# Eight chunk products of a pair of heads, issued head by head or with the two heads alternating

## The chip, the cores and the metric

The kernel runs on one core of a Trainium2 chip, in one launch. The metric is the device time of an execution in microseconds (us); a kernel's time is the median of its runs. The engines are TensorE (PE for its matmuls, PEld for its weight loads), VectorE (DVE), ScalarE (ACT), GpSimd (POOL) and SyncE (SP), which issues most DMAs. All arithmetic is in f32; the large products split their operands into two parts and issue three matmuls for one.

## What is computed

A network of two kinds of blocks over one sequence of 512 tokens with 1024 features: two blocks with a feed-forward part, a mixer of window attention and a convolution, another feed-forward part and a gate; then two blocks whose mixer has three branches side by side: a gated delta rule (6 heads), a sparse attention (6 heads) and a stick-breaking attention (4 heads). The change touches the gated delta rule alone. Its reference, cut to what matters (H = 6 heads, D = 64 features, chunks of C = 64 tokens, so n = 8 chunks):

```python
def gated_deltanet(q, k, v, z, a, b_logit, conv_w, a_log, dt_bias, norm_w):
    ...
    lower = jnp.where(strict, jnp.einsum('bhncd,bhnsd->bhncs', k_beta, k) * decay, 0.0)
    rhs = jnp.concatenate([v * beta[..., None], k_beta * jnp.exp(g)[..., None]], axis=-1)
    sol = lax.linalg.triangular_solve(lower, rhs, left_side=True, lower=True, unit_diagonal=True)
    u, w = jnp.split(sol, 2, axis=-1)
    attn = jnp.einsum('bhncd,bhnsd->bhncs', q, k) * decay

    def step(state, xs):
        q_i, k_i, u_i, w_i, g_i, a_i = xs
        v_new = u_i - jnp.einsum('bhcd,bhde->bhce', w_i, state)
        o_i = (jnp.einsum('bhcd,bhde->bhce', q_i * jnp.exp(g_i)[..., None], state)
               + jnp.einsum('bhcs,bhse->bhce', a_i, v_new))
        ...
    _, o = lax.scan(step, jnp.zeros((bsz, H, D, D), f32), xs)
```

Everything before the scan is independent for each chunk and each head.

## The kernel before

Features lie on partitions and tokens on columns, so a tile is [128, 512]. The class `Gdn` works on pairs of heads, j = 0, 1, 2: the first head of a pair on partitions 0 to 63, the second on 64 to 127, and the eight chunks side by side in 64 columns each. A product of one chunk of one head is therefore 64x64 times 64x64: it uses the upper or the lower half of TensorE's rows, and writes the same half of the partitions of one PSUM tile. `chunks8` (line 1368) issues such a product for every chunk of both heads, 16 in all; this text calls the 16 products a block. It is called from five places:

- `swap` (line 1460) transposes each head's chunks by a product with the identity. `cols` calls it for v, `pre` for k, and `gdn_mix` for the output of the scan.
- `pre` (line 1544) makes two blocks: U, the products of the chunk's keys with each other, and AT, those of queries and keys. VectorE multiplies both by the decay (line 1546).
- `mms` (line 1551) is called three times by `inverse`, for one level of the doubling of a triangular inverse: px, py and pyt. VectorE takes each result up (lines 1596, 1599, 1602).
- The end of `inverse` (line 1629) multiplies the inverse TT with the right-hand sides, which ScalarE copies out of PSUM (line 1630).

For a pair of heads that is 10 blocks, for the three pairs 30, and for the two calls of the mixer 60 blocks or 960 products. The last level of the inverse (`quarters`, line 1611) and the scan (lines 1643 to 1653) don't use `chunks8`; both issue the two heads in turn. In the scan each step has two such products for the state and two for the output.

The work beside this is large products of 128x128 by 128x512 (lines 259 to 261, `mm3`), for the next columns of the input projection, and the chain of the stick-breaking attention (lines 1169 to 1184). The program writes them as generators and takes steps from them between the small products (`pace`, `sparse`, `fill`, lines 737 to 782), so many for each block. A scheduler then sets the final order on each engine by when it estimates operands to be ready. `mms` hands the last of its 16 products to `pace`; this is the second head's last chunk in either order. Each weight tile of the large products comes by DMA on SyncE's queue and is split by ScalarE (line 232, wH) and VectorE (line 233, wL).

Of the kernel before, what the change touches and what calls it, by code (L numbers as in the profile page):

```python
# [16 lines left out]
PSUM = bass.MemoryType.PSUM  # L17
# [32 lines left out]
BLK = 16  # L50
# [15 lines left out]
class Vecs:  # L66
    """Column directory of the per-partition vectors."""
# [49 lines left out]
class Net:  # L117
# [15 lines left out]
    @contextmanager  # L133
    def phase(self, **tags):
        """Scratch: rotating [128, 512] tiles, so many of each tag. Phases nest."""
        old = self.tags, getattr(self, "tp", None)
        with self.tc.tile_pool(name="ph", bufs=1) as pool:
            self.tp = pool
            self.tags = {**old[0], **{k: v if isinstance(v, str) else (pool, v) for k, v in tags.items()}}
            yield  # L140
        self.tags, self.tp = old

    @contextmanager
    def psum(self, **tags):
        """PSUM banks, so many of each tag; or the tags that one goes round."""
# [60 lines left out]
    def weights(self, sources):  # L206
        """The [128, 1024] chunks of all weights, in the order of use."""
# [29 lines left out]
    def w(self):  # L237
        """The next 128-column tile of the weights."""
# [7 lines left out]
    def wraw(self, n):  # L246
        """The next n chunks of the weights as they are."""
# [15 lines left out]
    def mm2(self, out, l, r, **flags):  # L263
        """A narrow product in two halves of its rows, side by side in the array."""
# [9 lines left out]
    def lin(self, name, xs, tag="lin"):  # L274
        """The next product."""
# [6 lines left out]
    def lead(self, name, n, tag="lin", gain=None, norm=None, at=8, between=None):  # L282
        """The input of a step, its first products side by side, and the norm of the input."""
# [51 lines left out]
    def rstd(self, tiles, n, scale=1.0, adds=SQ_DVE):  # L335
        """1/sqrt(mean(x^2)+eps) over the features of x = scale * tiles: a row on every partition."""
# [17 lines left out]
    def rn(self, acc, n, scale=1.0):  # L354
        """By token, 1/sqrt of the mean over the partitions."""
# [8 lines left out]
    def rows(self, rn):  # L364
        """[128, 4] by token as a row on every partition."""
        return self.rows_end(*self.rows_in(rn))
# [48 lines left out]
    def rope_tables(self, pos, inv, sgn):  # L415
        """cos and signed sin of pos * inv, features on partitions."""
# [24 lines left out]
    def rope(self, ps, cos, sin, half, tag="q", tmp="t"):  # L441
        """ps * cos + swap(ps) * sin, the swap within each 32 partitions."""
# [9 lines left out]
    def mixer1(self, i):  # L452
# [7 lines left out]
        # taps by fours: their weights on the diagonals of [4 x 32, 32], a group of 32 features after the other  # L460
# [8 lines left out]
        for j in range(4):  # L469
# [6 lines left out]
            # the tile's groups of 32 features, 0 to 3 tokens late  # L476
# [19 lines left out]
        # in parts, stacked: [high, low] of a head against [high, high] of its keys  # L496
# [16 lines left out]
        def conv(j):  # L513
            """The convolution of tile j on the tensor engine, four taps at a time."""
# [134 lines left out]
    def ple(self, pT, gain, norm, last=False):  # L649
        """The gate's product, and beside it the tokens' rms-normalised projection with its gain."""  # L650
# [46 lines left out]
    def final_out(self, gain, out):  # L697
        """The last norm, by token."""
# [38 lines left out]
    def pace(self, inst, **rates):  # L737
        """Steps of the work that runs beside the current one, so many of each kind, but not ahead of
        the instruction of LAG calls before."""
# [11 lines left out]
    def sparse(self, cost):  # L751
        """Small products of a cost were issued: as many large ones belong beside them."""
# [7 lines left out]
    def fill(self, kind, n=1):  # L760
        """n steps of a kind, or all that are left."""
# [11 lines left out]
    def need(self, done, kind):  # L773
        """Steps of a kind until done."""
# [9 lines left out]
    def by_token(self, y):  # L784
        """PSUM: the tokens of y on partitions, [token, (block, feature)]."""
# [119 lines left out]
    def norm2_in(self, i, fin):  # L905
        """The input of the second block's mixer; after the first block, its last norm too."""
# [4 lines left out]
        def gates(gain):  # L911
            """Their few columns in four groups, each a fourth of the features."""
# [13 lines left out]
        def norm():  # L926
# [13 lines left out]
            # of the two norms together: (mean of the second's square + eps) / first's^2  # L940
# [9 lines left out]
    def rsqrt_ln(self, x, n, scale):  # L950
        """1/sqrt(scale * x + eps): exp of the logarithm, and one Newton step."""
# [10 lines left out]
    def head_norm(self, *args):  # L962
        """out = src / rms(src) over each 64 columns."""
# [16 lines left out]
    def to_mix(self, o, nt):  # L980
        """A token block, transposed."""
# [12 lines left out]
    def values(self, name, xs, rs):  # L994
        """The next columns, by token."""
# [58 lines left out]
    def nsa_split(self, d):  # L1054
        """Queries and keys in parts, stacked: [high, low] of a head against [high, high] of its keys."""
# [29 lines left out]
    def compress(self, i, d):  # L1085
        """The hidden units of the compressed keys and values."""
        nc = self.nc
        hids = []
        for nm in ("kc", "vc"):
            src = d[nm]  # L1090
            # pairs of tokens, with the positions' vectors in front (first half) and behind (second half)
# [34 lines left out]
    def compress2(self, d, w2):  # L1126
        """The keys and values from the hidden units."""
        nc, hids = self.nc, d["hids"]
        # each head's own part of the products, zero elsewhere: keys of two heads, values of four and of two query heads
# [17 lines left out]
    def sb(self, i, d, cr, G):  # L1147
        """Keys on partitions: log of the stick by a triangular product, then exp."""
# [48 lines left out]
    def nsa(self, i, d, G, mix, w2):  # L1197
# [44 lines left out]
        def add(n, po, f):  # L1242
            """A branch's part of the sum, and after the last one its norm."""
# [22 lines left out]
        def scores(n, br, hd):  # L1266
            """Selected (all blocks) and window (all tokens)."""
# [100 lines left out]
def chunks8(f):  # L1368
    """f of (a head's partitions, a chunk's columns), for every chunk of a pair of heads."""
    for _, s in H2:  # L1370
        for c in range(8):
# [3 lines left out]
class Gdn:  # L1375
    """Gated delta rule, in pairs of heads: on partitions a head's features or the tokens of a chunk (2 x 64)."""
# [12 lines left out]
    def gates_in(self, p):  # L1389
        """Gates, beta and the decay from a, by token."""  # L1390
# [14 lines left out]
        # softplus, cumulative over each chunk  # L1405
# [513 lines left out]
```

## Time and profile before

| | us |
|---|---|
| median of 3 runs | 3790.53 |
| lowest and highest run | 3789.84, 3797.76 |
| span of the profiled execution | 3791.1 |
| TensorE busy (matmuls) | 3723.9 |
| VectorE busy | 2311.5 |
| ScalarE busy | 1563.9 |

The profiled execution is told by its span, first instruction to last; it lies 0.6 us above the median of the runs. The first mixer of the second kind runs its gated delta rule from about 2060 to 2425 us of the span, the second from about 2940 to 3295.

How to read the rows further down: a group by line gives the line, the engine, the operation, what it writes and reads (out<-in), the shape and the number of records, then busy time, the mean length of one record in ns and the idle time ahead of it with what ended it. A timeline row gives the start in us, how long the row lasts, engine, line, operation, names, shape and the count of records in the row; a bracket tells of idle time ahead of it and who ended that. A row that holds several records lasts from the first start to the last end. One f32 matmul leaves two records, so 16 products are x32; a large product in the split type leaves one.

### The profile page before, as it was taken

Reading aid. Unit: us, or ns where it says so; the run is one execution under the profiler, and the core shown is the slowest. Engines: PE = TensorE matmul, PEld = TensorE weight load, DVE = VectorE, ACT = ScalarE, POOL = GpSimd, SP = SyncE. Lnnn points to the kernel's source line nnn. Section 1 sums busy time; section 2 is a strip of 40 time slices with the busy share of each in tenths; the row PEclk is TensorE's granted clock in tenths of the full one; section 3 lists DMA queues with packets and bytes.
Section 4 is the critical chain, followed back from the end, with each engine's and each line's share of the span. In section 5 each row is a group of like instructions: output and inputs, shape, how many; then the busy total and the mean of one; then the engine's idle time right before and its main releaser. Section 6 shows DMA issues by size and latency. Waiting matters only on the chain. (4 is left out here: it accounts for less than half of the span.)

```text
span 3791.1 us, 53948 instructions
## 1 busy us (share of the span) xinstructions
PE 3723.9 (98%) x20946; PEld 2919.5 (77%) x20946; DVE 2311.5 (61%) x4820; ACT 1563.9 (41%) x2974; POOL 147.2 (4%) x150
## 2 busy tenths in 40 slices
PE   9999999999999999999999999999999999999998
PEld 7888757888888885688887777778887777778887
DVE  5445556444743445753448876675667786676667
ACT  4233344333532334532345344553445344554345
POOL 1000000000100000100001000000001000000001
PEclk9999999999999998999999998999999999999999
DMA  3223312222322242122232111122323111122232
GB/s 132 99 95 101 106 40 89 95 100 95 100 95 100 95 127 64 52 98 100 95 100 94 68 40 68 40 100 95 100 95 134 51 40 62 46 90 100 95 100 84
DMA packets 97152, 329.85 MB, mean 87 GB/s; under 512 B 11008, under 2 KB 14976, under 8 KB 96896
## 3 DMA queue, kind: packets, MB, share of 16 engines
q1 hardware_dynamic: 90144, 311.96, 24.9%
q10 hardware_dynamic: 5472, 10.25, 0.8%
q0 software_dynamic: 1280, 4.20, 0.3%
q8 instruction: 164, 2.69, 0.3%
q14 instruction: 92, 0.75, 0.1%
HBM read 317.97 MB, written 8.39 MB: 86 GB/s over the span
## 5 line engine op out<-in xcount | busy, mean ns | idle before, releaser
L232 ACT CAST wH<-raw 128x512 fp32r<-128x512 f32 x1116 | 691.3, 620 | 1421.9 <-PE pgu L260 451.2
L233 DVE TENSOR_TENSOR wL<-raw,wH 128x512 fp32r<-128x512 f32 x1116 | 791.2, 710 | 590.4 <-ACT wH L232 558.2
L259 PE MATMUL pgu<-xH,wH 128*128 128x512 f32 x1408 | 549.5, 391 | 9.7 <-ACT wH L232 5.9
L260 PE MATMUL pgu<-xL,wH 128*128 128x512 f32 x1408 | 551.2, 391 | 6.1 <-DVE xL L313 6.1
L261 PE MATMUL pgu<-xH,wL 128*128 128x512 f32 x1408 | 550.7, 391 | 0.0
L259 PE MATMUL pd<-H,wH 128*128 128x512 f32 x1056 | 410.8, 389 | 0.0
L260 PE MATMUL pd<-L,wH 128*128 128x512 f32 x1056 | 410.8, 389 | 0.0
L261 PE MATMUL pd<-H,wL 128*128 128x512 f32 x1056 | 410.8, 389 | 0.0
L259 PEld LDWEIGHTS pgu<-xH,wH 128*128 128x128 f32 x1408 | 265.3, 188 | 65.2 <-ACT wH L232 5.9
L260 PEld LDWEIGHTS pgu<-xL,wH 128*128 128x128 f32 x1408 | 266.3, 189 | 62.2 <-DVE xL L313 6.7
L261 PEld LDWEIGHTS pgu<-xH,wL 128*128 128x128 f32 x1408 | 266.2, 189 | 55.4 <-DVE wL L233 0.2
L259 PE MATMUL pup<-xH,wH 128*128 128x512 f32 x704 | 274.8, 390 | 2.2 <-DVE h L895 1.2
L261 PE MATMUL pup<-xH,wL 128*128 128x512 f32 x704 | 274.0, 389 | 0.0
L260 PE MATMUL pup<-xL,wH 128*128 128x512 f32 x704 | 273.9, 389 | 0.0
L260 PEld LDWEIGHTS pd<-L,wH 128*128 128x128 f32 x1056 | 198.2, 188 | 41.1
L259 PEld LDWEIGHTS pd<-H,wH 128*128 128x128 f32 x1056 | 198.2, 188 | 41.1
L261 PEld LDWEIGHTS pd<-H,wL 128*128 128x128 f32 x1056 | 198.2, 188 | 41.1
L348 POOL TENSOR_TENSOR ssum<-ssum,sq 128x512 f32<-128x512 f32 x72 | 110.6, 1536 | 2674.7 <-ACT sq L347 2673.3
L259 PEld LDWEIGHTS pup<-xH,wH 128*128 128x128 f32 x704 | 132.1, 188 | 31.5 <-DVE h L895 2.0
L261 PEld LDWEIGHTS pup<-xH,wL 128*128 128x128 f32 x704 | 132.1, 188 | 27.6
L260 PEld LDWEIGHTS pup<-xL,wH 128*128 128x128 f32 x704 | 132.1, 188 | 27.1
L1344 DVE SCALAR_TENSOR_TENSOR y<-x,vecs,y 128x511 f32<-128x511 f32 (+1 forms) x176 | 131.3, 750 | 17.1 <-ACT y L1341 14.3
(568 smaller groups left out, 6108.0 us busy)
## 6 DMA issues: line engine op xcount, KB each, us to landing
raw<-ffn SPq DMA_DIRECT2D x395, 512.0 KB, 3.2
raw<-w_in SPq DMA_DIRECT2D x82, 512.0 KB, 3.2
raw<-w_out SPq DMA_DIRECT2D x40, 512.0 KB, 3.2
raw<-w_ple_gate SPq DMA_DIRECT2D x40, 512.0 KB, 3.2
away<-h ACTq DMA_DIRECT2D x16, 256.0 KB, 2.1
raw<-cmp SPq DMA_DIRECT2D x8, 512.0 KB, 3.3
h<-away POOLq DMA_DIRECT2D x16, 256.0 KB, 5.1
h<-xT SPq DMA_DIRECT2D x8, 256.0 KB, 6.5
```

What stands on the lines that cost most here:

```text
L232: nc.scalar.copy(H, r)
L233: nc.vector.tensor_tensor(L, r, H.bitcast(F32), OP.subtract)
L259: nc.tensor.matmul(ps, w[0], x[0], start=first, stop=False)
L260: nc.tensor.matmul(ps, w[0], x[1], start=False, stop=False)
L261: nc.tensor.matmul(ps, w[1], x[0], start=False, stop=last)
L348: (nc.vector if k >= adds else nc.gpsimd).tensor_tensor(acc, acc, q, OP.add)
L1344: nc.vector.scalar_tensor_tensor(y[:, s:], x[:, :T - s], w[:, f * 3 + tap:f * 3 + tap + 1], y[:, s:], OP.mult, OP.add)
```

## The change

`chunks8` swaps its two loops: the chunk becomes the outer one and the head the inner one. Each of the 960 products is still issued, with the same operands and the same output, and the first and the last product of a block are the same as before. The rest of the diff takes out comments and docstrings and moves later lines by one, so line 1551 becomes 1552 and so on.

```diff
 def chunks8(f):
-    """f of (a head's partitions, a chunk's columns), for every chunk of a pair of heads."""
-    for _, s in H2:
-        for c in range(8):
+
+
+    for c in range(8):
+        for _, s in H2:
             f(s, slice(c * 64, c * 64 + 64))
```

In the built order, the rows of a block read alike before and after, since the names and shapes of both heads' products are the same; 16 products in a row are one row. Where the scheduler sets other work between them, it shows. On TensorE, at the first pair of heads of the first mixer, at the end of `inverse` (puw are the right-hand sides times the inverse, psk and pv columns of the input projection), there stands before:

```order
L261 MATMUL psk<-xH,wL 128x512
L259 MATMUL psk<-xH,wH 128x512
L1629 MATMUL puw<-vb,TT 64x64 x16
L1629 MATMUL puw<-TT,kbg 64x64 x16
L260 MATMUL psk<-xL,wH 128x512
L261 MATMUL psk<-xH,wL 128x512
```

and now:

```order
L261 MATMUL psk<-xH,wL 128x512
L259 MATMUL psk<-xH,wH 128x512
L1630 MATMUL puw<-vb,TT 64x64
L260 MATMUL psk<-xL,wH 128x512
L1630 MATMUL puw<-vb,TT 64x64 x15
L1630 MATMUL puw<-TT,kbg 64x64 x16
L261 MATMUL psk<-xH,wL 128x512
```

One large product has moved between the first product of the block, which is the first head's, and the second, which is now the second head's. VectorE writes TT's last quarter for the first head and for the second head in two instructions (line 1625).

On TensorE, at the second pair of heads of the first mixer, the same products among the stick-breaking attention's (sbz); before:

```order
L261 MATMUL pnsa<-xH,wL 128x512
L1629 MATMUL puw<-vb,TT 64x64 x7
L1182 MATMUL sbz<-SH_17996,cr 128x384
L1629 MATMUL puw<-vb,TT 64x64 x9
L1629 MATMUL puw<-TT,kbg 64x64
L1182 MATMUL sbz<-SL_17999,cr 128x384
L1182 MATMUL sbz<-SHL_17997,cr 128x256 x2
```

and now:

```order
L261 MATMUL pnsa<-xH,wL 128x512
L1630 MATMUL puw<-vb,TT 64x64 x11
L1182 MATMUL sbz<-SH_17996,cr 128x384
L1630 MATMUL puw<-vb,TT 64x64 x5
L1630 MATMUL puw<-TT,kbg 64x64
L1182 MATMUL sbz<-SL_17999,cr 128x384
L1182 MATMUL sbz<-SHL_17997,cr 128x256 x2
```

The block is cut at the same instruction of the attention, but four products later. Cuts of this kind are in both orders at nearly the same places: 68 runs of such products before, 70 now. On TensorE, at the first block of `mms` in the first mixer, nothing but the line numbers changes; now:

```order
L259 MATMUL pqkv<-xH,wH 128x512
L1515 MATMUL row<-RS,sel 128x512 x2
L1552 MATMUL px<-T,UA 64x64 x16
L1515 MATMUL row<-RS,sel 128x512 x2
L260 MATMUL pqkv<-xL,wH 128x512
```

The orders of SyncE and GpSimd are the same as before; on VectorE and ScalarE a few instructions near such cuts change places.

## Rows read from the trace of the kernel before

**Rows 1.** Page, parts 1 and 2: busy us of each engine; TensorE's clock in tenths

```profile
PE 3723.9 (98%) x20946; PEld 2919.5 (77%) x20946; DVE 2311.5 (61%) x4820; ACT 1563.9 (41%) x2974; POOL 147.2 (4%) x150
...
PEclk9999999999999998999999998999999999999999
```

**Rows 2.** Groups by line and shape, TensorE: busy us, mean ns | idle before

```profile
L1460 PE MATMUL psw<-ident,y 64*64 64x64 f32 x384 | 24.4, 230 | 3.8 <-DVE rs L325 3.3 <-DVE y L1447 0.5
...
L1551 PE MATMUL px<-T,UA 64*64 64x64 f32 x192 | 11.4, 221 | 0.0
```

**Rows 3.** Timeline of TensorE, a block alone: start, us, engine, line, names, count

```profile
2128.69 1.90 PE L1551 MATMUL px<-T,UA 64*64 64x64 f32 x32
2130.52 0.50 PE L1514 MATMUL row<-RS,sel 8*128 8x512 f32 x2
```

**Rows 4.** Timeline of TensorE, two adjoining blocks and the next work

```profile
2141.76 1.72 PE L1551 MATMUL py<-X,TT 64*64 64x64 f32 x29
...
2145.09 0.50 PE L259 MATMUL psq<-xH,wH 128*128 128x512 f32 x1
```

**Rows 5.** Timeline of TensorE, alternating products: the scan, and the sum at line 266

```profile
2210.44 0.33 PE L1643 MATMUL pvd<-S,kbg 64*64 64x64 f32 x4
2210.60 0.28 PE L1647 MATMUL pgo<-S,qe 64*64 64x64 f32 x4
2210.82 0.70 PE L1169 MATMUL sbz<-sq,sk 64*128 64x256 f32 x2
...
2232.38 1.39 PE L266 MATMUL sbo<-sv,A 128*64 128x64 f32 x40
2233.70 0.50 PE L260 MATMUL pnsa<-xL,wH 128*128 128x512 f32 x1
```

**Rows 6.** Timeline of TensorE, two pieces of a block that is cut

```profile
2225.93 0.91 PE L1551 MATMUL pyt<-TT,X 64*64 64x64 f32 x12
2226.77 0.44 PE L1182 MATMUL sbz<-SH,cr 128*128 128x384 f32 x1
...
2228.42 0.44 PE L1551 MATMUL pyt<-TT,X 64*64 64x64 f32 x4
2228.79 0.50 PE L259 MATMUL pnsa<-xH,wH 128*128 128x512 f32 x1
```

**Rows 7.** Stretches: length, busy us (records) of each engine, clock, DMA share, GB/s

```profile
2120.00:2140.00 20.00, 19.65 (x218) 15.78 (x216) 18.34 (x47) 6.25 (x11) 0.52 (x1) 1.00 0.24 80
...
2184.00:2302.00 118.00, 117.85 (x1158) 87.59 (x1156) 90.48 (x240) 54.78 (x117) 5.16 (x13) 1.00 0.17 59
```

**Rows 8.** Timeline of VectorE, 2093 to 2128 us

```profile
2093.44 0.69 DVE L233 TENSOR_TENSOR wL<-raw,wH 128x512 fp32r<-128x512 f32 x1 [3.35 <-PE pqkv L261]
...
2122.68 0.42 DVE L1455 TENSOR_TENSOR vb<-psw,facT 128x256 f32<-128x256 f32 x1 [0.28 <-PE psw L1460]
...
2127.27 0.75 DVE L1509 SCALAR_TENSOR_TENSOR RS<-prt,c,R 96x512 fp32r<-96x512 f32 x1 [0.29 <-ACT R L1508]
```

**Rows 9.** Waits of VectorE, 2141 to 2302: us, times, longest

```profile
DVE vn L1645 <- PE pvd L1643: 6.9, 6, 5.0
DVE TT L1602 <- PE pyt L1551: 5.3, 2, 3.4
```

**Rows 10.** Stretches behind the blocks: PE, PEld, DVE, ACT, POOL, clock, DMA share, GB/s

```profile
2312.00:2339.00 27.00, 27.00 (x147) 16.37 (x146) 10.25 (x40) 8.37 (x26) 0.52 (x1) 0.50 0.00 1
...
3192.50:3199.00 6.50, 6.50 (x33) 4.09 (x33) 3.10 (x9) 1.31 (x6) 0.00 (x0) 0.50 0.27 81
```

**Rows 11.** Timeline of TensorE, first and last row of that work in each mixer

```profile
2299.98 0.50 PE L260 MATMUL pkc<-xL,wH 128*128 128x512 f32 x1
...
2364.95 0.68 PE L1460 MATMUL psw<-ident,UA 64*64 64x64 f32 x8
...
3179.86 0.50 PE L259 MATMUL pz<-xH,wH 128*128 128x512 f32 x1
...
3236.85 0.44 PE L1460 MATMUL psw<-ident,UA 64*64 64x64 f32 x4
```

## The prediction

> **What bounds the kernel now.** I read the page's first two parts, then the groups by line and shape, then the timeline of TensorE around the products that the change touches, then the stretches and the timeline of VectorE around the same times. TensorE is busy for 3723.9 of 3791.1 us, and its granted clock is full nearly throughout [rows 1]. A busy figure alone proves little, since matmuls overlap, so the reader should look at the timeline: where one group of matmuls ends, the next one starts without idle time [rows 3, 4, 6]. So TensorE's own stream sets the time, and what the change is worth is the time that the changed products take from that stream.
>
> The products are those issued through `chunks8`: lines 1460, 1544, 1551 and 1629. Nine groups carry them, with 1920 records in all: one of 384, as the first of [rows 2], and eight of 192, as the second. A product of f32 leaves two records, so there are 960 products, or 60 blocks of 16 (30 in each of the two calls of the mixer). The mean of 221 to 230 ns in these rows is the length of one record with its overlap; it is not what a product costs. The cost is the distance between starts. A block standing alone starts at 2128.69 and the next work on TensorE starts at 2130.52: **1.83 us** [rows 3]. Its 32 records span 1.90 us, so their starts lie (1.90 - 0.22)/31 = 54 ns apart. Two adjoining blocks take 2145.09 - 2141.76 = **3.33 us** [rows 4].
>
> **What the change does to a block.** It adds and removes no instruction; it changes which product follows which. Before, eight products of the first head (partitions 0 to 63) run in a row, then eight of the second (64 to 127); after, the two heads alternate. The trace already has alternating products of the very same shape, in the scan: lines 1643 and 1647 issue first one head, then the other. Their two pairs, 8 records, start at 2210.44 and the next work starts at 2210.82: 0.38 us. The four records of one group span 0.28 us, where four records at 54 ns would span 0.38 [rows 5]. A longer alternating run, of two halves of 64 columns, is the sum over values at line 266: 40 records take 2233.70 - 2232.38 = 1.32 us [rows 5]. From 8 records to 40 the time grows by 0.94 us, which is 29 ns for a record, against 54. So I take 0.38 us for the first 8 records and 29 ns for each further one, the start and the end of a run included:
>
> - A block alone: 0.38 + 24 x 0.029 = 1.08 us in place of 1.83, saving **0.75**.
> - Two adjoining blocks: 0.38 + 56 x 0.029 = 2.00 in place of 3.33, which I round to a saving of **1.30**.
> - A block that other work cuts into pieces: before, pieces of 12 and 4 records took 0.84 and 0.37 [rows 6]; by the same line they take 0.50 and about 0.26, saving 0.34 and 0.11 for half of a block. I take **0.60** for a whole one, since every piece pays its start and end anew.
>
> In the order of before, 29 blocks stand alone, 18 stand in nine adjoining pairs, and 13 are cut. The sum on TensorE's stream is 29 x 0.75 + 9 x 1.30 + 13 x 0.60 = 21.8 + 11.7 + 7.8 = **41.3 us**. The order of the changed kernel cuts the blocks at nearly the same places: 70 pieces in place of 68. In each mixer one block of line 1629 gets a large product between its first product and the other 15, because the second product reads the half of TT that VectorE writes second, and where before eight products of the first head hid that second write, now one does. This costs one more short piece, 0.2 to 0.3 us each, and I count it in the rounding above.
>
> **A rule weighed against the rows.** In the scan the two heads' products write the same PSUM tile, one head its lower and one its upper 64 partitions, and they overlap [rows 5]. The Trainium skill, "TensorEngine Tiling (Array Packing)", section Restrictions and Gotchas, says that different row tiles cannot access the same PSUM bank simultaneously. By that rule the alternating heads would take turns at the bank, a block would stay near 1.83 us and the sum would be near zero. The trace disagrees for this pairing of tiles, since the scan's pairs overlap within one bank; so I keep the rule only as a rival with a small chance.
>
> **What of the 41.3 us reaches the end.** A shorter block helps only if what comes after it is ready sooner too. Three places:
>
> - At 2093.44 VectorE ends a wait of 3.35 us for a large product that stands right behind the two blocks of line 1544 [rows 8]. This wait shortens by what the blocks save, so the gain passes on.
> - From there to 2128 VectorE is nearly without a gap; in 2120 to 2140 it is busy 18.34 of 20 us [rows 7]. The block at 2120.75 can give VectorE only the waits that it ends: 0.28 us before vb and, through the transposes and ScalarE, 0.29 us before RS [rows 8]. So 0.57 of 0.75 passes: 0.18 is lost, twice in the program.
> - In 2184 to 2302 TensorE is busy 117.85 of 118 us and VectorE 90.48 [rows 7]. Ten blocks there save some 6.6 us; VectorE would then be busy 90.48/111.4 = 81%. VectorE's longest waits from 2141 on are for TensorE, 6.9 and 5.3 us [rows 9], so it mostly follows. Still, dependent work now arrives up to 0.75 us sooner after its operand is asked for, and some of it will wait.
>
> The trace cannot price that last item. From below it is 0: VectorE and ScalarE wait for TensorE and simply move forward. From above it is half of the sum, 20.6 us, as if all stretches were like 2120 to 2140. I take 4 us, a tenth, nearer to the lower end, because the stretch 2120 to 2140, where VectorE is the one that is full, holds five of the first mixer's 30 blocks. With the 0.4 us above, 41.3 - 4.3 = **37 us** remain. No DMA is moved, and the queues of SyncE and GpSimd have the same order as before; VectorE and ScalarE change places of a few instructions only.
>
> Against the profiled execution's span, 3791.1, this is 3754.1; the median of the runs lies 0.6 us lower, so the forecast is **3753.5 us**.
>
> **The clock.** After the blocks of each mixer comes a stretch of small products in which the granted clock falls to 0.50 (1.2 GHz) although TensorE shows no idle time: 27 us in the first mixer, 6.5 in the second [rows 10]. The same work, from the first large product behind the last block of line 1629 to the next block of line 1460, takes 2364.95 - 2299.98 = 65.0 us in the one and 3236.85 - 3179.86 = 57.0 in the other [rows 11]. So 20.5 us more at the lower clock cost 8.0 us, 0.39 us for each. The change shifts these stretches in time, and either mixer could draw the long or the short fall. I expect no shift on average and put 8 us on either side.
>
> **The rivals.**
>
> - The wait moves to VectorE and ScalarE (chance 12%): half of the sum is lost, 3790.5 - 20.6 = 3770. For it: VectorE at 92% in 2120 to 2140 [rows 7]. Against: its waits for TensorE are the longest elsewhere [rows 9].
> - No overlap (5%): the heads take turns, at the bank or at the weight loads, and blocks stay as they are, or order and diff say "alternating" while the array serialises; about 3790. For it: the quoted rule. Against: the scan's pairs [rows 5].
> - Slower (3%): denser small products drop the clock in the chunk stretches themselves. The price is 0.39 us for each us at 1.2 GHz, so 95 us of it eat up the gain; if the stretches 2120 to 2184 and their counterparts in the second mixer, 128 us, all fell, it would be 3753.5 + 50 = 3803. For it: the fall in a stretch of small products [rows 10]. Against: the stretches with the blocks as they are run at full clock, and the same columns pass in less time.
>
> **How the numbers follow.** The forecast (clock either way, loss from 0 to 10 us) has 80% and spans 3742 to 3766; the first rival adds up to 3770. The range 3742 to 3770 therefore leaves out the two other rivals and part of the first. A difference under 0.2% (7.6 us) cannot be told from no change by such runs. Faster by more than that: 80 + 12 = 92%. Same: 5%. Slower: 3%.
>
> **What would show it.** In the changed kernel a block alone should take 1.0 to 1.2 us to the next work's start, its 32 records spanning about 1.15; two adjoining blocks 2.0. If these hold and the time has fallen by less than 30 us, new idle time on TensorE in 2090 to 2300, ended by VectorE or ScalarE, would name the loss. If a block still takes 1.8 us, the overlap is what I had wrong. If the clock row shows a longer or shorter fall in the two stretches, 0.39 us for each us is the clock's and not the order's.

## The result, and the profile after

| | before | changed |
|---|---|---|
| median, us (lowest to highest of 4 runs) | 3794.15 (3789.84 to 3799.39) | 3746.99 (3738.36 to 3755.17) |
| span of the profiled execution, us | 3791.1 | 3743.9 |
| mean granted clock of that execution | 0.984 | 0.986 |

The changed kernel takes 0.988 of the time of the kernel before (95% interval 0.9859 to 0.990), 47 us less. The forecast was 3753.5, with 3742 to 3770 as its range: the median lies inside, 6.5 us below the forecast. That 6.5 us is the interesting part, and most of the experiments are about it.

The page, parts 1 and 2, of the changed kernel (busy us of each engine; TensorE's clock in tenths), as in [rows 1]:

```profile
PE 3676.5 (98%) x20946; PEld 2876.1 (77%) x20946; DVE 2309.9 (62%) x4820; ACT 1563.8 (42%) x2974; POOL 147.8 (4%) x150
...
PEclk9999999999999998999999998999999999999999
```

Take TensorE's busy time from the span, before and after: 3791.1 - 3723.9 = 67.2 us idle, then 3743.9 - 3676.5 = 67.4. The record counts are the same on every engine, VectorE and ScalarE are as busy as before, and TensorE idles no longer. So the whole 47.2 us came out of TensorE's busy time, and next to nothing came back as waiting.

The timeline of TensorE in the changed kernel (start, us, engine, line, names, count): a block alone and two adjoining blocks, each with the next work behind it, as in [rows 3, 4]:

```profile
2119.40 1.15 PE L1552 MATMUL px<-T,UA 64*64 64x64 f32 x32
2120.48 0.59 PE L1515 MATMUL row<-RS,sel 8*128 8x512 f32 x2
...
2129.75 1.15 PE L1552 MATMUL py<-X,TT 64*64 64x64 f32 x32
2130.73 1.10 PE L1552 MATMUL pyt<-TT,X 64*64 64x64 f32 x32
2131.76 0.50 PE L259 MATMUL psq<-xH,wH 128*128 128x512 f32 x1
```

The block alone takes 2120.48 - 2119.40 = 1.08 us (1.83 before), the pair 2131.76 - 2129.75 = 2.01 (3.33 before). The same view at the block of the right-hand sides, whose first product stands apart now, and at a cut block, as in [rows 6]:

```profile
2145.11 0.33 PE L1630 MATMUL puw<-vb,TT 64*64 64x64 f32 x2
2145.37 0.50 PE L260 MATMUL psk<-xL,wH 128*128 128x512 f32 x1
...
2208.05 0.91 PE L1552 MATMUL pyt<-TT,X 64*64 64x64 f32 x22
2208.89 0.45 PE L1182 MATMUL sbz<-SH,cr 128*128 128x384 f32 x1
2209.26 0.45 PE L1552 MATMUL pyt<-TT,X 64*64 64x64 f32 x8
2209.64 0.50 PE L1182 MATMUL sbz<-SH,cr 128*128 128x512 f32 x1
```

Pieces of 22 and 8 records take 0.84 and 0.38 us; the split-off product takes 0.26. The groups by line (busy us, mean ns | idle before), as in [rows 2]:

```profile
L1461 PE MATMUL psw<-ident,y 64*64 64x64 f32 x384 | 15.5, 236 | 3.6 <-DVE rs L325 3.3 <-DVE y L1448 0.3
...
L1552 PE MATMUL px<-T,UA 64*64 64x64 f32 x192 | 6.9, 221 | 0.0
```

The mean length of a record has hardly changed (236 and 221 ns against 230 and 221), so it does not show the gain; what has changed is the distance between the records' starts. Over the nine groups busy time fell from 119.8 to 76.8 us. Measured as the distance from each of the 1920 records to the next start on TensorE, which leaves the overlap with the following work out, it fell from 109.7 to 68.6: **41.1 us**.

What is left, 47.2 - 41.1 = 6.1 us, has to come from something that shortens busy time elsewhere. Rows that both kernels share ahead of the first block show that it is not the change: the first block stands at 2071.57 us before and at 2065.15 after, so 6.4 us were gained before anything different had run. The granted clock differs there, in stretches of the window attention whose instructions are the same in both: up to 2060 us of the span, 61 us stand at 1.2 GHz before and 48 after.

### The profile page after: what moved, and what is told of

Its sections match the earlier page's. It is cut to its first block, busy times and chain, and to the rows that moved or that the text cites. A ratio compares the mean times of both kernels' runs of the same rounds, so it can differ in the third digit from the quotient of the medians.

```text
span 3743.9 us, 53944 instructions
## 1 busy us (share of the span) xinstructions
PE 3676.5 (98%) x20946; PEld 2876.1 (77%) x20946; DVE 2309.9 (62%) x4820; ACT 1563.8 (42%) x2974; POOL 147.8 (4%) x150
## 5 line engine op out<-in xcount | busy, mean ns | idle before, releaser
L259 PEld LDWEIGHTS pd<-H,wH 128*128 128x128 f32 x1056 | 198.2, 188 | 41.1
L261 PEld LDWEIGHTS pd<-H,wL 128*128 128x128 f32 x1056 | 198.2, 188 | 41.1
L260 PEld LDWEIGHTS pd<-L,wH 128*128 128x128 f32 x1056 | 198.2, 188 | 41.1
```

What stands on the lines that cost most here:

```text
L259: nc.tensor.matmul(ps, w[0], x[0], start=first, stop=False)
L260: nc.tensor.matmul(ps, w[0], x[1], start=False, stop=False)
L261: nc.tensor.matmul(ps, w[1], x[0], start=False, stop=last)
```

## The experiments

Besides the medians I use two numbers of each run, its time and its mean granted clock, because the runs of one kernel differ by their clock. In 80 runs of the kernel before, a clock of 0.979 goes with 3804 us and one of 0.988 with about 3781; the line through all of them falls by 2.8 us for each 0.001. A clock lower by 0.001 over 3790 us is 7.6 us more at 1.2 GHz, so one us at 1.2 GHz costs 2.8/7.6 = 0.37 us. Moving every run along that line to a clock of 0.986 makes kernels comparable to about 1 us, less well where the clock lies far from 0.986: the 18 runs of the changed kernel taken alone fall by 3.2 us for each 0.001, which at a clock of 0.991 makes a difference of 2 us.

| kernel | runs | median us | mean clock | mean at clock 0.986, us (standard error) |
|---|---|---|---|---|
| before | 80 | 3793.8 | 0.9836 | 3786.4 (0.2) |
| changed | 18 | 3744.0 | 0.9868 | 3744.5 (0.3) |
| order changed within a head | 10 | 3795.0 | 0.9832 | 3786.1 (0.6) |
| alternating at line 1552 alone | 6 | 3775.9 | 0.9852 | 3773.0 (0.6) |
| changed, with 180 large products | 5 | 3775.2 | 0.9896 | 3784.5 (0.6) |
| changed, with 14 large products in waits | 4 | 3730.2 | 0.991 | 3744.5 (0.8) |
| changed, with 30 large products at the same places | 5 | 3727.7 | 0.9936 | 3748.2 (0.3) |

### The changed kernel once more

> The changed kernel once more, unchanged. Theory: the 60 blocks give TensorE's stream 41.1 us, which all reaches the end, and the other 6 us between the two profiled spans (47.2 in all) are the clock's, since 7 us of them lie ahead of the first changed product. Then a block alone again takes 1.08 us and an adjoining pair 2.01 us, but the stretches at half clock differ from those of the first profile, in the window attention near 450 us above all, and the time is 3744 to 3756, the difference to the kernel before 41 to 47 us. Rival: the 6 us belong to the change; then the same stretches fall at the same places again and the difference is 47 us once more.

Its median is 3741.12 us (4 runs, 3732.79 to 3751.2), 0.9857 of the kernel before (0.9838 to 0.9877). The time lies below the 3744 to 3756 that I had written and the difference by medians, 55 us, above the 41 to 47, but the profiled run shows the blocks as before (1.08 and 2.01 us) and its clock stretches elsewhere: near 450 us of the span the clock was low for 27 us, where the first profile of the same kernel has 10. So the extra time moves from run to run, which speaks against the rival. At equal clock the difference is 3786.4 - 3744.5 = **41.9 us**, give or take 0.8 (95%), against 41.1 us on TensorE's stream.

### Another order, but within a head

```diff
-    for c in range(8):
-        for _, s in H2:
+    for _, s in H2:
+        for c in (0, 4, 1, 5, 2, 6, 3, 7):
             f(s, slice(c * 64, c * 64 + 64))
```

> The order of a block's products is changed as well, but within a head: chunks 0, 4, 1, 5, 2, 6, 3, 7 of the first head, then of the second, so that neighbours share the half of the rows. Theory (only products on different halves of the rows overlap): a block alone takes 1.83 us as in the kernel before, and the time is that of the kernel before within 4 us, 3790 to 3798. Rival (what helps is that neighbours write distant columns of the bank or that the scheduler placed other work anew): a block takes 1.1 us and the time is near 3750.

3794.95 us, ratio 0.9995 (0.9983 to 1.0008). The timeline of TensorE, with a block alone and the work behind it:

```profile
2126.03 1.90 PE L1552 MATMUL px<-T,UA 64*64 64x64 f32 x32
2127.86 0.50 PE L1515 MATMUL row<-RS,sel 8*128 8x512 f32 x2
```

1.83 us, the same as [rows 3]. Shuffling the products, and with it the scheduler's order around them, brings nothing; what counts is that neighbours belong to different heads, and so lie in different parts of the array.

### A part of the blocks

The transposes, `pre` and the right-hand sides call a copy of the old `chunks8`; `mms` alternates:

```diff
+def chunks8_heads(f):
+    for _, s in H2:
+        for c in range(8):
+            f(s, slice(c * 64, c * 64 + 64))
...
-        chunks8(lambda s, c: self.nc.tensor.matmul(p[s, c], x[s, c], self.N.ident[s, s], start=True, stop=True))
+        chunks8_heads(lambda s, c: self.nc.tensor.matmul(p[s, c], x[s, c], self.N.ident[s, s], start=True, stop=True))
...
```

> The heads alternate in the three products of the inverse's level alone (line 1552 of the changed kernel, 576 of the 1920 records); the transposes, the two products with the decay and the right-hand sides go head by head. In the two traces these 576 records take 33.0 and 20.5 us of TensorE's stream. Theory (the stream bounds, every saved us passes on, blocks add up): 12.5 us less than the kernel before, near 3781. Rival (a part of each saving is lost to waits of VectorE, which takes up these three results one after the other): 6 us or less. Second rival (the whole gain needs all blocks, since some other engine is late between them): within 3 us of the kernel before.

3775.91 us, ratio 0.9946 (0.9931 to 0.9962): 20 us by medians, but 3786.4 - 3773.0 = 13.4 us at equal clock, where TensorE's stream gives 12.5. The blocks add up, and their savings pass on; both rivals fall. A reader who had only the medians would have put some 6 us too much on these blocks.

### The price of an order by itself

Behind the last output stand runs of 64 products in one order each, separated by 30 large ones. An excerpt, the alternating run with a PSUM tile for each half of the rows:

```diff
+        for _ in range(4):
+            for c in range(8):
+                for p, s in ((X, up), (Y, dn)):
+                    nc.tensor.matmul(p[s, C[c]], mo[s, C[c]], mo[s, C[7 - c]], start=True, stop=True)
+        wide(30)
```

> The changed kernel, and behind its last output 64 products of 64x64 by 64x64 in f32 in each of six orders, with 30 large products between them, so that the price of an order stands by itself in the trace; their results are not used. Each has 128 records. (1) Head by head, 8 and 8: at 54 ns a record 6.9 us. (2) The two row halves alternating, one PSUM tile: at 29 ns 3.7 us. (3) The same with a PSUM tile for each half: 3.7 us if the bank plays no part, clearly less than (2) if the shared bank costs anything. (4) Two of one half, two of the other: 3.7 us if a product waits only for its own half, 5.3 us if only every second change overlaps. (5) The two row halves alternating, both writing partitions 0 to 63, each its own PSUM tile: 3.7 us if different rows suffice, 6.9 us if the output halves must differ too. (6) One row half, the two output halves alternating: 6.9 us if different rows are needed, 3.7 us if different output halves suffice. The whole is slower than the changed kernel by what is appended, some 100 us.

The timeline of TensorE: head by head (line 745; four of its records stand ahead of the warm-up), alternating (750), two by two (761), one row half with alternating output halves (771). Then the group rows (busy us, mean ns) of the two orders with two PSUM tiles, which the timeline lists record by record: line 755 alternating rows and output halves, line 766 alternating rows with one output half:

```profile
3769.53 6.19 PE L745 MATMUL mX<-o 64*64 64x64 f32 x124
3775.64 7.09 PE L739 MATMUL mZ<-mr,onesr 128*128 128x512 f32 x30
3782.67 3.95 PE L750 MATMUL mX<-o 64*64 64x64 f32 x128
3786.55 7.10 PE L739 MATMUL mZ<-mr,onesr 128*128 128x512 f32 x30
...
3804.48 4.00 PE L761 MATMUL mX<-o 64*64 64x64 f32 x128
3808.41 7.11 PE L739 MATMUL mZ<-mr,onesr 128*128 128x512 f32 x30
...
3826.35 3.95 PE L771 MATMUL mW<-o 64*64 64x64 f32 x128
3830.23 7.10 PE L739 MATMUL mZ<-mr,onesr 128*128 128x512 f32 x30
```

```profile
L766 PE MATMUL mX<-o 64*64 64x64 f32 x64 | 3.9, 219 | 0.0
L755 PE MATMUL mX<-o 64*64 64x64 f32 x64 | 3.9, 219 | 0.0
```

Head by head 124 records take 6.11 us to the next work, 49 ns each where I had expected 54. Alternating, 128 take 3.88, 30 ns each. Three readings follow. A second PSUM tile changes nothing (3.9 busy either way), so the bank that both heads share costs nothing here. Two by two takes 3.93, hardly more than strict alternation. And the surprise is the last run: products on the same 64 rows that write different halves of the partitions overlap just as well, 3.88 us where I had written 6.9. It is not the rows that must differ; the quadrant of the array must.

> The changed kernel, and behind its last output four more orders of products with rounds of large products between them; their results are not used. (1) 64 products of 64x64 by 64x64 that go round all four quadrants (rows 0 to 63 or 64 to 127, output partitions 0 to 63 or 64 to 127), a PSUM tile for each half of the rows: 3.9 us if one stream of columns at 30 ns a record is the bound, 2 us if each quadrant works on its own. (2) Head by head, neighbours writing two PSUM tiles in turn: 6.1 us or more if the shared quadrant is what serialises, 3.9 us if it is the shared PSUM tile. (3) Head by head with 128 columns, 32 products: if a product costs by its columns, 64 records at 107 ns, 6.8 us. (4) The same alternating: half of (3), 3.4 us.

The timeline of TensorE: the first product that goes round four quadrants and the work behind the run; the first of the same quadrant with two PSUM tiles (line 752) and the work behind it; 128 columns head by head (757) and alternating (762):

```profile
3765.94 0.27 PE L747 MATMUL mX<-o 64*64 64x64 f32 x1
...
3767.85 7.09 PE L740 MATMUL mZ<-mr,onesr 128*128 128x512 f32 x30
3774.87 0.32 PE L752 MATMUL mW<-o 64*64 64x64 f32 x2
...
3781.22 7.09 PE L740 MATMUL mZ<-mr,onesr 128*128 128x512 f32 x30
3788.25 4.54 PE L757 MATMUL mW<-o 64*64 64x128 f32 x64
3792.71 7.14 PE L740 MATMUL mZ<-mr,onesr 128*128 128x512 f32 x30
3799.78 3.71 PE L762 MATMUL mW<-o 64*64 64x128 f32 x64
3803.42 7.14 PE L740 MATMUL mZ<-mr,onesr 128*128 128x512 f32 x30
```

Round four quadrants, 120 records (eight more stand ahead of the warm-up) take 1.91 us, 16 ns each. In the same quadrant a second PSUM tile does not help (6.35 us), so the quadrant serialises, not the tile. What each quadrant does shows where the timeline has a row for a product or a record: products of one head in two PSUM tiles (line 752, two records in a row), the two heads alternating (line 755 of the kernel with the six orders), and four quadrants in turn (747):

```profile
3775.16 0.28 PE L752 MATMUL mW<-o 64*64 64x64 f32 x2
3775.27 0.28 PE L752 MATMUL mV<-o 64*64 64x64 f32 x2
3775.39 0.28 PE L752 MATMUL mW<-o 64*64 64x64 f32 x2
...
3793.68 0.22 PE L755 MATMUL mX<-o 64*64 64x64 f32 x1
3793.69 0.22 PE L755 MATMUL mY<-o 64*64 64x64 f32 x1
3793.74 0.22 PE L755 MATMUL mX<-o 64*64 64x64 f32 x1
...
3766.05 0.22 PE L747 MATMUL mX<-o 64*64 64x64 f32 x1
3766.05 0.22 PE L747 MATMUL mY<-o 64*64 64x64 f32 x1
3766.06 0.22 PE L747 MATMUL mX<-o 64*64 64x64 f32 x1
3766.07 0.22 PE L747 MATMUL mY<-o 64*64 64x64 f32 x1
3766.11 0.22 PE L747 MATMUL mX<-o 64*64 64x64 f32 x1
```

In one quadrant four records take 3775.39 - 3775.16 = 0.23 us, one every 58 ns. In about the same time two records start with two quadrants in turn, and four with four: each quadrant keeps its pace and the others work beside it. The 49 ns of the run head by head, like the 54 of a block, already contain some overlap, since a few records of the two heads start within 4 to 6 ns of each other where the head changes: after every 16 records there, once in a block.

With 128 columns I was wrong twice: head by head costs 70 ns a record where I expected 107, and alternating 57 where I expected half of that. What limits the wider products the runs don't tell; the gain of alternation is 0.8 us of 4.5 there, against 2.4 of 6.3 for 128 records with 64 columns.

### The clock

> The changed kernel unchanged, for more runs with their mean granted clock and for one more clock row. So far 8 runs of it have a mean clock of 0.986 and 17 runs of the kernel before 0.983; read at one clock, 0.986, the two kernels stand at 3744.6 and 3787.0 us, 42.4 us apart, close to the 41.1 us of TensorE's stream. Theory A (the change itself leaves less time at half clock, since the stretches of small products are shorter): the mean clock again is 0.985 to 0.988, above that of the kernel before by 0.002 to 0.004. Theory B (the difference of the clocks was luck): the means of the two come within 0.001 of each other, and the difference of the times falls to 41 to 44 us.

> The kernel before, unchanged, for one more clock row and for the spread of its runs. Both theories: time as the kernel before, within 2 us. Theory A: the half-clock stretches behind the two mixers' blocks (27 and 7 us in the first profile) are there again, 30 us or more in all. Theory B: they come and go as the stretch near 450 us does, which was 27 us in two profiles and 10 us in four, with the same instructions.

The changed kernel: 3741.54 us (5 runs, 3737.51 to 3746.05), ratio 0.9858 (0.9843 to 0.9872). The kernel before: 3793.18, ratio 0.9992. The mean clocks stay apart. The half-clock stretch behind the second mixer's blocks is there in this profile of before too, 6.8 us, and absent in the changed kernel's. I took that for the place, and tested it:

> The changed kernel unchanged, for a fourth clock row. Three profiles of it show no half clock behind the last blocks of the second mixer (3140 to 3200 us), where both profiles of the kernel before and that with the order changed within a head show 7 us there. If that is the change's doing, it is missing here too, and the mean clock over the runs is again 0.985 to 0.988; if it was luck, some of it is back.

> The kernel before, unchanged, for its third clock row. If the head-by-head order is what lets the clock fall behind the last blocks of the second mixer (3185 to 3200 us here), the 7 us are there a third time; mean clock 0.982 to 0.985.

The changed kernel came to 3743.68 us (5 runs), the kernel before to 3792.34. The place did not hold: the fourth profile of the changed kernel has a fall of 20 us there, and the third profile of before one of 37. The same stretch in the first profile of the changed kernel (length; busy us and records of PE, PEld, DVE, ACT, POOL; clock; DMA share; GB/s):

```profile
3140.00:3200.00 60.00, 59.23 (x597) 42.47 (x596) 40.67 (x139) 29.62 (x89) 1.10 (x5) 1.00 0.16 54
```

and in the fourth:

```profile
3140.00:3200.00 60.00, 59.34 (x546) 41.96 (x546) 33.34 (x128) 25.00 (x80) 1.09 (x5) 0.83 0.17 54
```

The clock's total held: 0.9868 over 18 runs against 0.9836 over 80, a difference of 0.0032, give or take 0.0011 (95%), so 24 us less at 1.2 GHz, worth 0.0032 x 2800 = 9 us (6 to 12). Theory A is right on the sum, but that the shorter stretches do it is not shown. Up to 2060 us, where both kernels run the same instructions, the three profiles of the kernel before have 61 us at 1.2 GHz each and the four of the changed kernel 48, 58, 48 and 48; behind it they have 59, 66 and 90 against 59, 59, 59 and 64. So about half of the difference between these profiles lies where the change cannot act, and most of the rest is the one fall of 37 us. Why the mean clocks differ stays open.

> The changed kernel with three large products (128x128 by 128x512) ahead of each of the 60 blocks, into the PSUM tile that the block then overwrites: 180 products, 0.24 us each by the run with the separate orders, 42.7 us on TensorE's stream, about what the change saved. At equal clock that gives 3744.6 + 42.7 = 3787, the time of the kernel before, if the stream alone counts; less, if part of it goes into waits, which would show that the changed kernel has idle room. Theory A in the form that denser columns keep the clock up: mean clock 0.986 or above, time 3785 to 3788. If the length of the stretches is what counts: mean clock 0.983, time 3794 to 3797.

```diff
+    def large(self, p):
+        for _ in range(3):
+            self.nc.tensor.matmul(p, self.N.onesr, self.sel, start=True, stop=True)
...
         p = self.N.pat("psw")
+        self.large(p)
```

3775.24 us, ratio 0.9946 (0.993 to 0.9962). At equal clock it stands 3784.5 - 3744.5 = 40.0 us above the changed kernel, for 42.7 us of products: the stream is full, and even added work finds nearly no idle room. But its mean clock is 0.9896, so by the median it is 19 us faster than the kernel before although TensorE has about the same amount of work. With the added large products the mean clock is above 0.986, as theory A had it, and the time lower than the 3785 to 3788 that I had written. The stretch of this run behind the blocks of the first mixer, in the same columns:

```profile
2289.00:2326.00 37.00, 36.88 (x351) 25.37 (x350) 23.03 (x86) 20.07 (x59) 1.10 (x5) 1.00 0.13 45
```

And the stretch of the changed kernel that answers to it, and to the first of [rows 10]:

```profile
2289.00:2316.00 27.00, 27.00 (x147) 16.34 (x146) 10.14 (x39) 8.46 (x26) 0.53 (x1) 0.50 0.00 1
```

That is the same 27 us at 1.2 GHz as before the change, in this profile, and full clock with the added products until a fall of 3 us that begins at 2325.9. (The fourth profile of the changed kernel has 7 us there and the one with the order changed at line 1552 alone none, so one profile proves little; the mean of the runs is the evidence.)

If large products keep the clock up, they should be put where they cost little, into TensorE's waits. The timeline of the changed kernel shows such a wait at the start of a window attention:

```profile
1453.59 0.33 PE L545 MATMUL sc<-ks,qs 128*128 128x128 f32 x1 [1.08 <-DVE nm L549]
```

Some 2.5 us later the clock falls for 24 us. The next kernel puts 4 large products into that wait, into a PSUM tile that later work overwrites (and 3 into the start of each sparse attention):

```diff
+                    if n == 0 and hd in WARM:
+                        if 0 not in early:
+                            early[0] = self.out_ps()
+                        with self.tc.issue_after(last.ins):
+                            for _ in range(WARM[hd]):
+                                nc.tensor.matmul(early[0], self.onesr, ks[0], start=True, stop=True)
...
-            po = self.out_ps()
+            po = early.pop(0) if n == 0 and early else self.out_ps()
...
+WARM, WARM2 = {2: 4}, {1: 3}
```

> The changed kernel with a few large products (128x128 by 128x512) whose result is overwritten, where TensorE waits at the start of the four attention stretches behind which the granted clock falls: 4 behind the third score product of each window attention (TensorE stands idle there for 1.08 us) and 3 behind the second score product of each sparse attention (idle for 0.57 us in the first mixer). 14 products of 0.24 us are 3.3 us, of which about 2.5 fit into the idle time. Theory A (what lets the clock fall is a stretch in which TensorE idles and then has small products only): the falls of 10 to 27 us near 450, 24 near 1456 and 27 near 2283 us become shorter or go, up to 60 us at half clock in all; at 0.37 us for each that is up to 22 us for a cost of 1, so 3722 to 3738 us with a mean clock of 0.989 or more, against 3743 for the changed kernel. Theory B (the falls follow a rhythm of their own): same clock, 3743 to 3747 us.

**3730.22 us** (4 runs, 3729.84 to 3731.88), 0.9845 of the kernel before (0.9828 to 0.9863): the fastest kernel of the study that computes the whole network, 14 us below the changed kernel's median of 18 runs. The two did not run side by side: the kernel before had a median of 3787.83 us beside this one and of 3793 to 3796 beside the later runs of the changed kernel. Each held against the kernel before (by the means of the runs), the gain is about 10 us, give or take 6 (95%). At equal clock it stands level with the changed kernel (both 3744.5; 2 us above it by that kernel's own line), so the added products cost little, and the gain is the clock's, 0.991 against 0.9868. The timeline of TensorE in this kernel shows the four products in the former wait:

```profile
1452.60 1.19 PE L552 MATMUL po<-ks,onesr 128*128 128x512 f32 x4
1453.63 0.22 PE L545 MATMUL sc<-ks,qs 128*128 128x128 f32 x1
```

The stretch behind them, in this kernel:

```profile
1456.00:1480.00 24.00, 23.80 (x139) 10.40 (x138) 11.50 (x44) 12.01 (x50) 0.11 (x1) 1.00 0.19 44
```

and in the changed kernel:

```profile
1456.00:1480.00 24.00, 23.86 (x78) 9.36 (x81) 6.17 (x28) 7.56 (x33) 0.00 (x0) 0.50 0.00 1
```

139 records in place of 78 in the same 24 us, at full clock in place of half. The twelve profiles of this study without these products all have a fall here, of 3 to 24 us; the two with them have none. Of the three falls that theory A named, this is the only one that went in this kernel: near 450 us there are 10 us at 1.2 GHz, as in most profiles, and behind the first mixer's blocks 14, between the 27 and 7 of the changed kernel's profiles.

> As the run before it in this list, with 8 in place of 4 such products in each window attention and 7 in place of 3 in each sparse attention, 30 in all, so 7.1 us, of which about 2.5 fit into idle time. Theory A: still fewer us at half clock than with 14 of them, mean clock 0.990 or more; since the 16 added products cost 3.8 us, the time is lower than that of the run before only if they take away 10 us more at half clock. Theory B: same clock as the changed kernel, 3747 to 3750 us.

3727.66 us (5 runs, 3723.55 to 3729.28), mean clock 0.9936. In this kernel the later of the added products overwrite sums of the sparse attention that are still needed, so it measures time only. At equal clock it stands 3.7 us above the changed kernel (6 by that kernel's own line), about what its further products cost, and it gives that back by a still higher clock; 2.5 us better than the run before it, as theory A allows. Theory B falls with both.

## Why the prediction was right, point by point

- **What bounds.** TensorE's stream: right. Its idle time is 67.2 us before and 67.4 after, and 180 added products cost 40.0 of their 42.7 us.
- **The price of a block.** 1.08 us alone and 2.00 for a pair were forecast, 1.08 and 2.01 measured. The price came from the scan's pairs, which alternate as the blocks now do, and from the sum at line 266 [rows 5], whose products read all 128 rows and alternate in the half of the partitions that they write. That this alternation has the same price as that of the rows was taken for granted; only the kernel with the six orders shows it, 3.88 us for both. A cut block was put at 0.60 us where the rows quoted for it (0.45 for half of one) would give 0.90; the traces have about 0.6, so the choice was good, but those rows did not show it. The sum on the stream was 41.3 against 41.1. The split-off product of line 1630 costs 0.26, within its 0.2 to 0.3.
- **The rule on the PSUM bank.** The Trainium skill, "TensorEngine Tiling (Array Packing)", section Restrictions and Gotchas, says that different row tiles cannot access the same PSUM bank simultaneously. The runs decide against it for products that write different halves of the partitions: one PSUM tile and two give the same 3.9 us. Products on different rows that write the same partitions of one tile were not run. The same page, section Tiling Modes, has different tiles of a mode work in parallel: there the runs agree, with 16 ns a record on four quadrants against 58 within one. Keeping it as a rival of 5% was fair; the scan's rows had already shown the overlap.
- **The loss to waits.** Too large. I took 4.3 us; at equal clock the kernels differ by 41.9 us where the stream gives 41.1, so the loss is 0, within 0.8. No row had priced this term: a tenth of the sum was a choice between 0 and half. The reason that I gave for its lower end is what happens: VectorE waits for TensorE and moves forward. Its waits in the stretch that answers to [rows 9] (2127.5 to 2282 us; us, times, longest) have shrunk:

```profile
DVE vn L1646 <- PE pvd L1644: 5.9, 8, 3.8
...
DVE TT L1603 <- PE pyt L1552: 2.5, 2, 2.0
```

and the wait of 3.35 us at 2093.44 [rows 8] is shorter by 1.51, in the timeline of VectorE:

```profile
2084.85 0.69 DVE L233 TENSOR_TENSOR wL<-raw,wH 128x512 fp32r<-128x512 f32 x1 [1.84 <-PE pqkv L261]
```

- **VectorE in the tight stretch.** The forecast of a small loss at the block of 2120.75 is borne out in kind. The stretch that answers to the first of [rows 7] has VectorE busy for 18.97 of 19 us, and TensorE idle for 0.78 us where it was 0.35. A further saving there would mostly turn into waiting.

```profile
2110.60:2129.60 19.00, 18.22 (x226) 13.84 (x226) 18.97 (x50) 6.63 (x12) 0.53 (x1) 1.00 0.26 85
```

- **The clock.** The price was right, 0.39 us forecast and 0.37 measured for each us at 1.2 GHz; "no shift on average" was the step that failed. The changed kernel is granted 0.0032 more clock on average, 9 us, for a reason that stays open. I had asked of dense small products only whether they could make the clock fall (the 3% rival); on average it did not fall but rose. The blocks do not all run at full clock either: outside the stretches of [rows 7], the block at 2954.11 took 3.21 us before, and the same block 1.90 after, where 1.83 and 1.08 are the prices at full clock.
- **The number.** Of the 6.5 us between forecast and median, 4.3 are the loss that did not come and some 2 the clock: the forecast started from 3790.53 us, which by the line is a clock of 0.9845, and the four runs of the result had 0.9853, for which the line gives 3744.5 + 0.7 x 2.8 = 3746.5. That this median lay inside the range of 3742 to 3770 was in part luck: the next three of the same kernel are 3741.12, 3741.54 and 3743.68 us, two of them below its lower end, because the loss that did not come and the higher clock add up on the same side.
- **The rivals.** "No overlap" falls with the block's 1.08 us; "the wait moves" with the unchanged idle time; "slower" with the mean clock.

## What to carry to other kernels

In these runs, products of 64x64 by 64x64, each in a quarter of the array, cost little more than the busiest quadrant costs: issue products of different quadrants next to each other, and read from the distance between starts, not from the busy figure, what that gives. With 128 columns it gave far less, so measure it at the shape at hand. Where TensorE's stream was full, the saving on it passed on entirely, and the allowance for waits should come from places where another engine is shown to be full, not from a fraction of the sum. Before giving a cause for some 10 us of difference between two runs, read their granted clocks: here the clock alone spreads one kernel over 24 us, and a few large products in TensorE's waits went with a higher mean clock and some 10 us less.

## What the runs showed of the hardware

- Products of 64x64 by 64x64 in f32 start a record every 58 ns within one quadrant. Over a run, a record takes 49 ns head by head, 30 when two quadrants alternate, and 16 when four do; whether two quadrants differ in rows or in output partitions makes no difference, nor does sharing a PSUM tile when the written partitions differ.
- With 128 columns the change from head by head to alternating gives 57 ns against 70.
- Near 450 us of the span the changed kernel had the clock at 1.2 GHz for 10 us in one profile and for 27 in another, so one profile does not tell what a change does to the clock; means over runs do.
- The falls in the attentions come shortly after TensorE idled 0.6 to 1.1 us and went on with small products (128x128 by 128x128 in the window attention). With large products in that idle time the fall near 1456 us was gone, the one near 450 us stayed at 10 us in one kernel and was gone in the other, and the one behind the first mixer's blocks was 14 us and none.
